# A hybrid decoder layer on one core: new issue orders on all five queues, and the residual's x in the buffer of y

## The chip, the core and the metric

The kernel runs on one core of a Trainium2 chip. The metric is the device time in microseconds (us). The engines are called by their short names: PE (TensorE, matmuls), DVE (VectorE), ACT (ScalarE), POOL (GpSimd) and SP (SyncE, which here only issues DMAs).

## What is computed

One layer of a decoder trunk, 256 tokens of width 1024, all inputs and the output in float32:

```python
h = _rmsnorm(x, norm1_g[i])
proj = h @ w_in[i]
(q_a, k_c, v_c, k_s, v_s, k_w, v_w, g_nsa,
 q_b, k_b, v_b, g_ma, g_mb) = jnp.split(proj, SPLIT_POINTS, axis=-1)
...
y_a = _nsa_mixer(q_a, k_c, v_c, k_s, v_s, k_w, v_w, g_nsa, ...)
y_b = _dilated_mixer(q_b, k_b, v_b)
mixed = jax.nn.sigmoid(g_ma) * (y_a @ w_o_a[i]) + jax.nn.sigmoid(g_mb) * (y_b @ w_o_b[i])
x = x + mixed @ w_out[i]
h2 = _rmsnorm(x, norm2_g[i])
x = x + jnp.square(jax.nn.relu(h2 @ w_up[i])) @ w_down[i]
```

The first mixer attends over compressed, selected and windowed keys, the second over dilated keys; both are causal.

## The kernel before

**Pieces of weights.** Every weight is loaded in float32 pieces of 128 x 768 (384 KB; those of `kv_w` are 128 x 840, 420 KB) by `load_to` (L303 to L317), the first four (`kv_c`) from ACT's DMA queue, all others from SP's. `split_to` then makes two halves of each piece: a high half `wh`, which is a cast to the reduced type of the matmul (on ACT, L345; for piece 0 on DVE, L349), and a low half `wl`, which is what the cast left out (a subtraction on DVE, L350). A product of such a piece with activations, which are kept as two halves in the same way, takes three matmuls: high with high, low with high, high with low (L468 for the very first chunk, L479 to L481 for the other projections, L983 to L985 in `mm3` for gates, output projections and the MLP). So each piece costs one DMA, one ACT cast and one DVE subtraction before PE can use it.

**The start.** x comes in four parts, `xg0` to `xg3` (L314), with the gains of the first norm in front of `xg0`. `scale_x` (L412 to L416) makes the two halves of the scaled x, `hT0` on ACT (L415) and `hT1` on DVE (L416), one chunk `k` of 128 features at a time. `setup` (L422 to L448) squares x on ACT (L426, `sx`), adds the squares on POOL (L428), sums over features on PE (L432) and raises to the power -0.5 on POOL (L436, `rs`); the factor `rs` is applied to what the projections give, not to x. POOL also multiplies the rotary tables by the gains of the heads (L444 `ropeg`, L447). While x is on its way, PE runs ten warm-up matmuls on a tile of `ones` (L408), which POOL sets (L403).

**The middle and the end.** Until about 250 us the projections, both mixers and the gates are interleaved. The attention transposes its probabilities on PE (L709) into a high half (`phi`, ACT) and a low half (`plo`, DVE L714), read by L721 and L723. Each mixer writes into `y` (made at L1052); its last readers are the halves `yb` (ACT L959, DVE L960). Then x is needed a second time, for the residual: `x1` (made at L1100, one load of 1 MB at L1101) is read and rewritten by L1116, and L1117 and L1118 make the halves of `h2` from it. The up- and down-projection fill the rest, and L1175 to L1177 write the result.

**Who decides the order.** `ORDER` holds one list for each engine: numbers of instructions in the order in which they were written in the program, with `a+n` for a run of n of them. `issue_order` ties each engine's instructions together in that order; it adds no semaphore, so an engine takes its instructions in the listed order and each waits only for its own data. A DMA stands in the list of the queue that issues it. `once` makes a tile in the wrapper `Own`, which gives each tile its own buffer, whatever tag it is called with:

```python
    def tile(self, shape, dt, name, **_):
        self.n += 1
        return self.pool.tile(shape, dt, name=name, tag=f"{name}{self.n}", bufs=1)
```

In SP's list numbers 0 to 3 are the four parts of x, 4 to 7 the pieces of `kv_s`, 9, 16, 19 and 20 those of `kv_w`, 8 the identity matrix, 10 `gr` and 11 `rope` (gains and rotary table), 12 to 15, 17 and 18 small constants and masks, 21 to 103 further pieces, 104 the load of `x1`, 105 and on the pieces of the gates' and MLP's weights still to come.

Of the kernel before, what the change touches and what calls it, by code (L numbers as in the profile page):

```python
# [11 lines left out]
F32 = mybir.dt.float32  # L12
# [7 lines left out]
S = 256  # L20
# [100 lines left out]
1 0 2 4 3 9+2 104 15 13 12 16 11 19 14 20 18 5 17 6 8 7 21+83 105+60 166 165 167+4 172 171 173+5 179 178  # L121
180+4 185 184 186+4 191 190 192+5 198 197 199+2""",
    "ACT": """
# [15 lines left out]
474 473 475+3 479 478 481 480 482 484 483 485+3 489 488 491 490 492 494 493 495+3 499 498 501 500 502+38""",  # L139
    "DVE": """  # L140
# [20 lines left out]
635+2 634 637+4 643 641 644 642 645+4 650+2 649 652+2""",  # L161
    "PE": """
# [1124 lines left out]
```

## Time and profile before

| what | us |
| --- | --- |
| median of 3 runs | 458.88 (458.87 to 458.94) |
| the profiled execution | 458.8 |
| its span | 457.0 |
| PE busy | 445.6 (98%) |
| DVE busy | 358.0 (78%) |
| ACT busy | 284.2 (62%) |
| POOL busy | 83.7 (18%) |

All times inside the trace count from the start of the span. The span is a little shorter than the time of the execution, which holds what lies around it. The mean clock granted to PE is 0.993 of full speed. Busy shares are averages over the whole span; the windows further down split them by stage. A matmul is shown with its whole duration although the next one starts before it ends, so a busy PE can still be slower than it might be.

### The profile page before, as it was taken

The page shows a single profiled execution, that of the slowest core. Times are in us where ns is not written, and L with a number is a line of the kernel's source. Part 1 is how long each engine was busy: PE and PEld are TensorE (multiplying, and loading weights), DVE is VectorE, ACT ScalarE, POOL GpSimd, SP SyncE. Part 2 cuts the span into 40 slices and gives each one's busy share as a digit, 9 for nine tenths or more (in the row PEclk, how much of TensorE's full clock was granted, in tenths as well). Part 3 has the DMA queues.
Part 4 walks back from the last instruction along what each step waited for, and adds up shares of the span by engine and source line. Part 5 has one row for each costly group of instructions (what it writes and reads, how often), then busy time and mean ns, then how long its engine had stood idle before and what let it go on. Part 6 is the DMA issues. An engine that isn't in the chain of part 4 may idle for free.

```text
span 457.0 us, 9071 instructions
## 1 busy us (share of the span) xinstructions
PE 445.6 (98%) x3413; PEld 431.1 (94%) x3413; DVE 358.0 (78%) x654; ACT 284.2 (62%) x622; POOL 83.7 (18%) x92
## 2 busy tenths in 40 slices
PE   4999999999999999999999999999999999999996
PEld 4999899899999999898999999999999999999996
DVE  3989999999999998899999886886856654555440
ACT  4855677678999778876775555665665634433330
POOL 2712121313041000200000001796322300000000
PEclk9799999999999999999999999999999999999999
DMA  8974586725535522541521647666666667677620
GB/s 304 367 244 146 154 287 181 236 89 167 157 105 141 171 70 71 175 140 68 162 82 42 199 128 231 201 193 186 205 184 195 183 187 210 185 216 199 179 78 13
DMA packets 29484, 76.92 MB, mean 168 GB/s; under 512 B 3664, under 2 KB 5120, under 8 KB 29312
## 3 DMA queue, kind: packets, MB, share of 16 engines
q1 hardware_dynamic: 28864, 74.77, 54.7%
q10 hardware_dynamic: 576, 1.57, 1.0%
q8 instruction: 27, 0.44, 0.4%
q14 instruction: 17, 0.14, 0.1%
HBM read 75.28 MB, written 1.05 MB: 167 GB/s over the span
## 4 chain that ended last, share of the span: by engine, by line
PE 93%; DVE 2%; ACT 2%; DMA 2%; issue 0%; ACTq 0%
PE acc L983 19%; PE acc L985 19%; PE acc L984 19%; PE acc L480 6%; PE acc L481 6%; PE acc L479 6%; PE tp L709 3%; PE acc L468 2%; DMA raw<-in_kv_c 2%; PE sp L754 1%; PE pvo L721 1%; ACT wh L345 1%; PE pvo L723 1%; PE tp L552 1%; PE dsp L920 1%; PE hacc L615 1%
## 5 line engine op out<-in xcount | busy, mean ns | idle before, releaser
L350 DVE TENSOR_TENSOR wl<-raw,wh 128x768 fp32r<-128x768 f32 (+2 forms) x183 | 177.6, 979 | 61.7 <-ACT wh L345 57.2
L345 ACT CAST wh<-raw 128x768 fp32r<-128x768 f32 (+1 forms) x182 | 149.6, 833 | 102.1 <-PE acc L984 74.5
L983 PE MATMUL acc<-u,wh 128*128 128x256 f32 x256 | 71.6, 280 | 0.0
L984 PE MATMUL acc<-u,wh 128*128 128x256 f32 x256 | 71.6, 280 | 0.0
L985 PE MATMUL acc<-u,wl 128*128 128x256 f32 x256 | 71.5, 279 | 0.0
L984 PE MATMUL acc<-h,wh 128*128 128x256 f32 x256 | 69.0, 280 | 0.0
L983 PE MATMUL acc<-h,wh 128*128 128x256 f32 x256 | 69.0, 279 | 0.0
L985 PE MATMUL acc<-h,wl 128*128 128x256 f32 x256 | 66.1, 279 | 0.0
L480 PE MATMUL acc<-wl,hT 128*128 128x384 f32 (+1 forms) x164 | 55.1, 350 | 0.3 <-DVE wl L350 0.3
L479 PE MATMUL acc<-wh,hT 128*128 128x384 f32 (+1 forms) x164 | 54.7, 348 | 0.0
L481 PE MATMUL acc<-wh,hT 128*128 128x384 f32 (+1 forms) x164 | 54.6, 347 | 0.0
L1159 POOL TENSOR_TENSOR r<-r 128x256 f32<-128x256 f32 x32 | 27.7, 866 | 128.7 <-ACT r L1158 127.5
L985 PEld LDWEIGHTS acc<-u,wl 128*128 128x128 f32 x256 | 48.2, 188 | 0.0
L983 PEld LDWEIGHTS acc<-u,wh 128*128 128x128 f32 x256 | 48.1, 188 | 0.0
L984 PEld LDWEIGHTS acc<-u,wh 128*128 128x128 f32 x256 | 48.1, 188 | 0.0
L983 PEld LDWEIGHTS acc<-h,wh 128*128 128x128 f32 x256 | 47.6, 188 | 0.0
L984 PEld LDWEIGHTS acc<-h,wh 128*128 128x128 f32 x256 | 47.4, 188 | 0.0
L985 PEld LDWEIGHTS acc<-h,wl 128*128 128x128 f32 x256 | 45.8, 188 | 0.0
L502 POOL TENSOR_TENSOR st<-st,nhalf 128x6 f32<-128x6 f32 (+1 forms) x16 | 21.6, 1348 | 92.8 <-DVE st L501 65.7
L984 PE MATMUL acc<-hT,wh 128*128 128x256 f32 x128 | 36.1, 293 | 0.0
L985 PE MATMUL acc<-hT,wl 128*128 128x256 f32 x128 | 35.9, 293 | 0.0
L983 PE MATMUL acc<-hT,wh 128*128 128x256 f32 x128 | 35.1, 290 | 0.0
(212 smaller groups left out, 986.9 us busy)
## 6 DMA issues: line engine op xcount, KB each, us to landing
raw<-in_cells SPq DMA_DIRECT2D x128, 384.0 KB, 3.4
raw<-in_cw SPq DMA_DIRECT2D x10, 384.0 KB, 3.2
raw<-in_q_a SPq DMA_DIRECT2D x8, 384.0 KB, 3.8
raw<-in_q_b SPq DMA_DIRECT2D x8, 384.0 KB, 3.4
raw<-in_k_b SPq DMA_DIRECT2D x8, 384.0 KB, 3.2
raw<-in_v_b SPq DMA_DIRECT2D x8, 384.0 KB, 3.1
raw<-in_kv_w SPq DMA_DIRECT2D x4, 420.0 KB, 6.7
raw<-in_kv_c ACTq DMA_DIRECT2D x4, 384.0 KB, 7.0
```

The source lines that it names most:

```text
L345: nc.scalar.copy(hi[:, :m], src)
L350: nc.vector.tensor_sub(lo[:, :m], src, f(hi[:, :m]))
L468: nc.tensor.matmul(acc[t][:, :n], hT[h][:, k, t * 128:(t + 1) * 128], w[:, kk * n:(kk + 1) * n], start=h == 0 and k == 0 and w is hi, stop ...
L479: nc.tensor.matmul(o, hT[0][:, k, ts], hi[:, c], start=k == 0, stop=False)
L480: nc.tensor.matmul(o, hT[0][:, k, ts], lo[:, c], start=False, stop=False)
L481: nc.tensor.matmul(o, hT[1][:, k, ts], hi[:, c], start=False, stop=k == 7)
L502: nc.gpsimd.tensor_tensor(st[:, 1, :h], st[:, 0, :h], nhalf[:, :h], op=OP.pow)
L709: nc.tensor.transpose(pt[0:rows, i * 128:(i + 1) * 128], s, ident)
L983: nc.tensor.matmul(o, hi, a[0][k], start=start, stop=False)
L984: nc.tensor.matmul(o, hi, a[1][k], start=False, stop=False)
L985: nc.tensor.matmul(o, lo, a[0][k], start=False, stop=stop)
L1159: mul = nc.gpsimd.tensor_mul(r, r, r)
```

## The change

Two lines of `hybrid_layer` give `y` and `x1` one buffer, by taking them from the pool itself with one tag; and all five lists of `ORDER` are replaced by other permutations of the same instructions.

```diff
-    st_["y"] = once([128, 8, S], F32, "y")
+    st_["y"] = big.pool.tile([128, 8, S], F32, name="y", tag="y", bufs=1)
...
-    x1 = big.tile([128, 8, S], F32, name="x1", tag="y", bufs=1)
+    x1 = big.pool.tile([128, 8, S], F32, name="x1", tag="y", bufs=1)
```

```diff
     "SP": """
-1 0 2 4 3 9+2 104 15 13 12 16 11 19 14 20 18 5 17 6 8 7 21+83 105+60 166 165 167+4 172 171 173+5 179 178
-180+4 185 184 186+4 191 190 192+5 198 197 199+2""",
+0+5 9 8 11 10 12 16 19 14 17+2 13 20 15 5+3 21+80 104 101+3 105+60 166 165 167+4 172 171 173+5 179 178 180+4
+185 184 186+4 191 190 192+5 198 197 199+2""",
     "ACT": """
-0+4 6 10 13 9 4+2 7+2 11 16 15 14 17 12 19+2 25+4 18 21 47 22 24 35 48 36 23 49 38 41 37 58 42 29+2 32+2 43
...
+0+4 6 4+2 9 13 7+2 10 14 11 16 15 12 17 20 25 19 26+3 18 21+2 35+2 23 50 24 38 51+2 47 58 32 54 48+2 37 43
...
     "POOL": """
-28 25 2 15 14 0+2 7 3+3 11+2 10 9 8 6 13 18 17 16 19+3 23+2 22 26+2 34+2 38 37 40 29 39 30 33 31 36 32 42 41
...
+0+3 14+2 25 28 7 9 3 8 4 13 5 11 10 12 6 19 18 17 16 20+2 24 22+2 27 34+2 26 37 29 38 40 39 30 33 36 31+2
...
```

What the numbers at the start of these lists are. SP: the load of `x1` moves from the eighth place to the 102nd, just before the last three pieces that are loaded ahead of the MLP's; `xg0` goes ahead of `xg1`, `xg3` ahead of the first piece of `kv_s`, and the identity, `rope` and `gr` come earlier. ACT: behind its four loads (0 to 3) stands the cast of the second `kv_c` piece (6) in both; before, the square of `xg1` (10), the cast of the third piece (13), the square of `xg0` (9) and then the scalings of x (4, 5, 7, 8) follow; after, the scalings 4 and 5, the square of `xg0`, the cast of the third piece, the scalings 7 and 8, the square of `xg1`. DVE: the first two halves `hT1` come before the low half of the third piece, no longer behind it. POOL: `nhalf` and `ones` (0, 1) come first, before the other memsets, and the products of `ropeg` (8, 9, 13) alternate with the adds of the squares (3, 4, 5), behind which they all stood before. PE: the ten warm-up matmuls and the first chunk's products stay first; products of the first token half and the second are grouped otherwise, and the sums L432 move from the places 43 to 57 to the places 84 to 87. In the up-projection PE's new list runs straight as written, where the old one still exchanges neighbours; the down-projection is straight in both. In between, every list is permuted throughout. One example, which the prediction takes up: the low half `plo` whose reader is PE's instruction number 705 moves ten places ahead in DVE's list (from 349 to 339), and that reader 89 places ahead in PE's (from 1172 to 1083).

## Rows read from the trace of the kernel before

**Rows 1.** Waits of PE; columns: engine, line, awaited, us in total, times, longest.

```profile
PE acc L468 <- ACT hT L415: 4.1, 1, 4.1
PE acc L408 <- POOL ones L403: 2.4, 1, 2.4
PE tp L536 <- ACT kc L646: 0.3, 1, 0.3
```

**Rows 2.** Windows; columns: stretch, length, busy PE, PEld, DVE, ACT, POOL, PEclk, DMA, GB/s.

```profile
2.45:7.03 4.58, 4.58 (x20) 4.34 (x20) 1.59 (x3) 1.28 (x1) 0.05 (x1) 1.00 0.95 336
7.03:11.12 4.09, 0.00 (x1) 0.01 (x1) 1.91 (x3) 3.18 (x6) 0.51 (x2) 0.89 1.04 413
11.12:17.20 6.08, 6.08 (x19) 5.74 (x20) 6.08 (x8) 6.03 (x12) 4.16 (x3) 0.51 1.04 391
17.20:20.00 2.80, 2.80 (x20) 2.80 (x18) 2.80 (x4) 1.44 (x2) 1.56 (x2) 1.00 1.00 357
...
20.00:180.00 160.00, 159.23 (x1072) 149.84 (x1072) 152.10 (x324) 119.92 (x316) 29.66 (x26) 1.00 0.54 164
180.00:250.00 70.00, 69.79 (x560) 65.54 (x559) 65.59 (x142) 50.61 (x119) 2.81 (x3) 1.00 0.36 108
```

**Rows 3.** Costliest groups; columns: line, engine, operation, count, busy us, mean ns, idle before.

```profile
L984 PE MATMUL acc<-u,wh 128*128 128x256 f32 x256 | 71.6, 280 | 0.0
...
L984 PE MATMUL acc<-hT,wh 128*128 128x256 f32 x128 | 36.1, 293 | 0.0
```

**Rows 4.** Timeline of the first 24 us; columns: start, us, engine, line, operation, idle before.

```profile
0.72 0.98 POOL L870 MEMSET pc<- 48x512 f32 x2 [0.29 <-POOLq L1277]
...
6.98 0.19 POOL L440 COPY g<-xg 128x8 f32<-128x8 f32 x1 [4.58 <-DMA xg<-in_xg]
...
7.52 0.83 ACT L345 CAST wh<-raw 128x768 fp32r<-128x768 f32 x1 [3.39 <-DMA raw<-in_kv_c]
8.26 0.63 ACT L426 ACTIVATE sx<-xg 128x512 f32<-128x512 f32 x1
8.39 0.96 DVE L350 TENSOR_TENSOR wl<-raw,wh 128x768 fp32r<-128x768 f32 x1 [1.75 <-ACT wh L345]
...
9.30 0.83 ACT L345 CAST wh<-raw 128x768 fp32r<-128x768 f32 x1 [0.42 <-DMA raw<-in_kv_c]
...
10.16 0.96 DVE L350 TENSOR_TENSOR wl<-raw,wh 128x768 fp32r<-128x768 f32 x1 [0.82 <-ACT wh L345]
10.57 0.89 ACT L415 ACTIVATE hT<-xg 128x256 fp32r<-128x256 f32 x2
...
11.12 3.13 PE L468 MATMUL acc<-wh,hT 128*128 128x384 f32 x8 [4.09 <-ACT hT L415]
...
14.05 1.16 PE L468 MATMUL acc<-wl,hT 128*128 128x384 f32 x3
...
15.71 1.46 POOL L428 TENSOR_TENSOR sx<-sx,sx 128x512 f32<-128x512 f32 x1 [1.23 <-ACT sx L426]
15.95 2.99 DVE L350 TENSOR_TENSOR wl<-raw,wh 128x768 fp32r<-128x768 f32 x2
```

**Rows 5.** Tile y, its last reader on DVE: ns min/median/max, first and last start.

```profile
L960 DVE SCALAR_TENSOR_TENSOR yb<-y,yb x2: 415/420/426, 238.8 to 244.9; 128x256 fp32r<-128x256 f32 x2
```

**Rows 6.** Tile x (`x1` in the program): first reader, and its load to landing.

```profile
L1116 DVE TENSOR_TENSOR x<-acc,x x8: 424/425/426, 262.9 to 274.0; 128x256 f32<-128x256 f32 x8
...
DMA to landing us min/median/max: 8.9/8.9/8.9
```

**Rows 7.** Timeline of DVE and of PE, 255 to 261 us: the piece loaded next.

```profile
255.51 0.95 DVE L350 TENSOR_TENSOR wl<-raw,wh 128x768 fp32r<-128x768 f32 x1
...
260.46 0.40 PE L985 MATMUL acc<-mT,wl 128*128 128x256 f32 x2
```

**Rows 8.** Timeline of DVE and of PE, 186 to 189 us: the low half `plo`.

```profile
186.26 0.68 DVE L714 TENSOR_TENSOR plo<-tp,phi 128x512 fp32r<-128x512 f32 x1
...
188.61 0.42 PE L723 MATMUL pvo<-plo,vSW 128*64 128x512 f32 x1
```

More of the change, by code (lines that the diff above doesn't have):

```diff
@@ L120 @@
     "SP": """
-1 0 2 4 3 9+2 104 15 13 12 16 11 19 14 20 18 5 17 6 8 7 21+83 105+60 166 165 167+4 172 171 173+5 179 178
-180+4 185 184 186+4 191 190 192+5 198 197 199+2""",
+0+5 9 8 11 10 12 16 19 14 17+2 13 20 15 5+3 21+80 104 101+3 105+60 166 165 167+4 172 171 173+5 179 178 180+4
+185 184 186+4 191 190 192+5 198 197 199+2""",
     "ACT": """
[15 rows of a table removed]
-474 473 475+3 479 478 481 480 482 484 483 485+3 489 488 491 490 492 494 493 495+3 499 498 501 500 502+38""",
-    "DVE": """
[20 rows of a table removed]
-635+2 634 637+4 643 641 644 642 645+4 650+2 649 652+2""",
-    "PE": """
[60 rows of a table removed]
-2575+17 2597 2592+3 2598 2595 2599+20 2620 2619 2621+767""",
[15 rows of a table added]
+484 483 485+3 489 488 491 490 492 494 493 495+3 499 498 501 500 502+38""",
+    "DVE": """
[20 rows of a table added]
+637+4 643 641 644 642 645+4 650+2 649 652+2""",
+    "PE": """
[49 rows of a table added]
+1907+280 2188+17 2187 2205+1183""",
     "POOL": """
-28 25 2 15 14 0+2 7 3+3 11+2 10 9 8 6 13 18 17 16 19+3 23+2 22 26+2 34+2 38 37 40 29 39 30 33 31 36 32 42 41
-45+5 44 50+5 56 55 57+4 62 61 63+11 43 74+14""",
+0+3 14+2 25 28 7 9 3 8 4 13 5 11 10 12 6 19 18 17 16 20+2 24 22+2 27 34+2 26 37 29 38 40 39 30 33 36 31+2
+41+14 56 55 57+4 62 61 63 65 64 66 68 67 69+19""",
 }
```

177 rows, old and new, of the table ORDER are left out of this document.

## The prediction, made before the changed kernel was run

> **What bounds the kernel now.** I read the waits of TensorE (PE) first [rows 1]: its only long waits are 2.4 us for a memset before the warm-up matmuls and 4.1 us for `hT` before the first projection matmul; no other is longer than 0.3 us. Then the windows [rows 2]: from 11.12 on PE is busy almost throughout (159.23 of 160.00 us between 20 and 180, 69.79 of 70.00 between 180 and 250). So what is issued first decides the start, and afterwards only a change of pace or a new hold can move the end. The tail after the last matmul holds the same instructions in both kernels, and I price it at no change.
>
> Busy is not the same as full pace, though. VectorE (DVE) is busy 152.10 of 160.00 us between 20 and 180 [rows 2], and matmuls that read fresh halves are a little longer there: 293 ns with `hT` against 280 with `u` [rows 3]. With 128 calls in each of three such lines (the other two 293 and 290), that is 128 x (13 + 13 + 10) ns = 4.6 us of small holds inside "busy". This is where a new order can gain or lose besides the start.
>
> The profiled execution reports 458.8 us for a span of 457.0; the median of the runs is 458.88, which is 0.08 more. The sum is made on 458.8. A measurement of this kernel tells changes above 0.2%, 0.92 us, from none.
>
> **Part 1, the start.** Before, ScalarE (ACT) waits until 7.52 for the second `kv_c` piece, casts it, squares `x` (0.63), waits 0.42 for the third piece, casts it (0.83), squares again and scales the first chunk of `x` only at 10.57; PE starts at 11.12 [rows 4]. In the new ACT list both first `hT` scalings stand directly behind the first cast. Consecutive ACT instructions overlap slightly, the next starting about 0.1 before the end shown, as the square at 8.26 did. So the scaling starts at 8.26, and PE starts as long after it as before, 11.12 - 10.57 = 0.55: at 8.81 instead of 11.12, a gain of **2.31**. The data for it is there: `xg0`, which also holds the gains, had landed by 6.98, where a POOL copy waited for it, and is now issued ahead of `xg1`. The squares, the third cast and POOL's adds that move behind the scaling feed `rs`, which no matmul of the first projection reads.
>
> **Part 2, three stumbles.** In 11.12 to 17.20 PE issues 19 matmuls [rows 2], one every 6.08 / 19 = 0.32. The first eight reach from 11.12 to the start of the ninth at 14.05 [rows 4]: 2.93 - 8 x 0.32 = **0.37** lost, at the matmuls that read the low half `hT1`, which DVE makes after the low half of the third piece (10.16 + 0.96 = 11.12). DVE's list now has the first pair of `hT1` ahead of that, right behind the low half of the second piece (8.39 + 0.96 = 9.35). I take the 0.37 as gained; the bounds are 0 and 0.37.
>
> **Part 3, the clock.** The granted clock is 1.00 during the warm-up, 0.89 over the idle stretch 7.03 to 11.12, 0.51 from 11.12 to 17.20 and 1.00 after [rows 2]; 0.51 is the lower of the two levels, 1.2 GHz. The lower level costs 6.08 x (1 - 0.51) = 2.98 us. POOL's new list puts the `ones` memset, for which PE waited 2.4 us [rows 1], second instead of seventh. POOL's memsets start at 0.72 [rows 4]; behind one short one it is done by about 1.0, an estimate. The warm-up then starts about 1.4 earlier, and with its 4.58 ends at 5.6; PE then idles 5.6 to 8.81, 3.2 us against 4.09 before. No row shows whether the shorter gap spares the drop, so its worth lies between 0 and **2.98**. I take 0: a gap of the same kind, only a fifth shorter, is nearest to the one shown. It stays the largest term that may turn out better.
>
> **Part 4, x for the residual.** The 1 MB load of `x1` leaves SP's list at 7.52 and moves ahead of the last three pieces before the mixers end. At the 391 GB/s of 11.12 to 17.20 [rows 2] its megabyte takes 2.7 us, so the loads queued behind it (`kv_w1` and on) land up to 2.7 earlier. Before, that was hidden: DVE was busy 6.08 of 6.08 and 2.80 of 2.80 there. Now it covers the earlier start of PE, so I book no gain; without it the start would be partly given back. At the new place the load waits for the last reader of `y`, DVE's `yb` at 244.9 + 0.42 = 245.3, and lands 2.7 to 8.9 later (its price alone at that rate, and issue to landing of the copy before): 248.0 to 254.2. Its first reader is at 262.9, a margin of 8.7 us or more [rows 5, 6]. The three `cells` pieces behind it in SP's queue wait with it: at 384 KB, 1.0 us each by the same rate, the first is there by 249.0 to 255.2. DVE makes its low half at 255.51, and PE reads that at 260.46 [rows 7], 4.0 after DVE's end at 256.46; even the late bound, with a cast like the 0.83 of rows 4 and the 0.95 of DVE behind it, gives 257.0 and leaves 3.5. Price 0.
>
> **Part 5, the other 430 us.** All five lists are permuted far into the up-projection. No instruction is added or removed, and PE's work is the same. The bounds are a gain of the 4.6 us of holds [rows 3] and a loss, worked out as rival C. I take 0, since the holds come from DVE, whose sum of work is unchanged and which has only 160.00 - 152.10 = 7.9 us of idle to give.
>
> **Sum:** 458.8 - 2.31 - 0.37 = 456.1, and with the 0.08 to the median **456.2 us**.
>
> **Rivals.** A: the clock does not drop, or DVE's work arrives better ordered in the middle. The first alone gives 456.2 - 2.98 = 453.2; half the holds alone, 2.3, give 453.9. I price this case at **453.5**. For it speaks that both sources are real time in the rows; against it that nothing in DVE's load is removed.
>
> B: DVE cannot follow. It was idle 1.75 before 8.39 and 0.82 before 10.16 [rows 4]; its first work still waits for the same landings, and only most of that 0.82, about 0.6, is recovered. If the holds of the middle are all DVE's, PE falls back on DVE's schedule and 458.88 - 0.6 = **458.3** remains, no change by measurement. What feeds this: POOL's `ropeg` products now stand between its adds and so fall into the time in which DVE makes low halves. Beside a POOL add that starts at 15.71, two DVE low halves take 2.99 where one alone takes 0.96 [rows 4], so about 1.1 lost to one meeting; two or three such meetings moved into the start eat the 2.31. By the Trainium skill, page "SBUF — State Buffer", section "🔬 SBUF: two separate sides", VectorE and GpSimd share one pair of ports as an exclusive lock, and the one that starts first keeps it for its whole instruction. By that rule, with which the row of 2.99 agrees, the total lost is the same as before and only its place moves.
>
> C, the other sign: PE's list runs ahead of DVE's at the attention. The low half `plo` of the transposed probabilities is done at 186.26 + 0.68 = 186.94 and read at 188.61, a slack of 1.67 [rows 8]. In the new lists it stands 10 places earlier on DVE, worth 10 x 152.10 / 324 = 4.7, but its reader stands 89 places earlier on PE, worth 89 x 69.79 / 560 = 11.1 [rows 2]. PE would get there 11.1 - 4.7 - 1.67 = 4.7 too soon, and it starts 2.7 earlier besides while DVE gains 0.6 at the start: 6.8 to make up. DVE can make it up from its 7.9 us of idle, if the new order fills nearly all of it. If it fills only 2.0, PE is held 4.8 and the time is 456.2 + 4.8 = **461.0**. The deciding point is 4.1 us of idle filled, at which the wait equals the 2.7 gained; below it the kernel is slower. Against it: places are not time, and other waits before 180 may already have been shortened by the same reordering.
>
> SP held up by the shared buffer would also make it slower, but only if `y`'s last reader came over 3.5 us later than now; I give that no chance of its own.
>
> **Chances.** Forecast 0.54, own range 454.9 to 457.6 (the 0.37 and part of a meeting on one side, half of the clock's cost on the other); A 0.20; B 0.11; C 0.15. Faster by over 0.2% (below 457.96) takes the forecast and A: 0.74; within 0.2% B: 0.11; slower C: 0.15. The range reaches over A's 453.2 to B's upper end, 459.0, and leaves out C and a little below: **453.0 to 459.0**.
>
> **What would show it.** Right: first `hT` on ACT near 8.3 and PE's first L468 near 8.8; a low clock stretch of about 6 us following it; no wait of L1116 for a DMA; SP's `x1` issue at 243 to 246; PE still without long waits. Wrong: PE starting at 9.5 or later because the second `kv_c` piece lands later; PE waits for `plo`, `phi` or `wl` of some us between 140 and 200 (C); PE pitch above 0.17 around 17 to 40 with DVE full (B); or no 0.51 stretch at all (A).

## The result: slower, and the profile after

The changed kernel takes **463.99 us** in the median (462.46 to 464.5, 4 runs) against 458.88 (458.44 to 458.94): ratio 1.0108, 95% interval 1.0083 to 1.0132, slower by 1.1%. The forecast was 456.2 with a range to 459.0. The profiled execution took 464.11 with a span of 462.1, so the two profiles differ by 5.1 us of span. All lines of the program have moved up by 11 (L468 is now L457, L350 is L339, L428 is L417).

The busy line of the page after, then its waits of PE, in the columns of [rows 1]:

```profile
PE 449.1 (97%) x3413; PEld 433.0 (94%) x3413; DVE 360.2 (78%) x654; ACT 284.5 (62%) x622; POOL 86.4 (19%) x92
```

```profile
PE acc L457 <- ACT hT L404: 3.4, 1, 3.4
PE acc L469 <- DVE wl L339: 2.5, 1, 2.5
PE hacc L602 <- DVE blk L589: 1.7, 1, 1.7
PE acc L397 <- POOL ones L392: 1.0, 1, 1.0
PE pvo L710 <- DVE plo L703: 0.2, 1, 0.2
```

Two of [rows 1] are shorter, and two new waits on DVE have come, 4.2 us together. The windows, in the columns of [rows 2], say when:

```profile
9.00:12.00 3.00, 3.00 (x11) 3.00 (x11) 2.60 (x6) 3.00 (x6) 0.00 (x0) 0.50 1.04 392
...
20.00:60.00 40.00, 35.82 (x210) 33.83 (x209) 35.43 (x67) 20.68 (x39) 9.44 (x10) 0.96 0.48 149
...
24.90:28.30 3.40, 3.34 (x10) 3.20 (x11) 2.85 (x4) 2.87 (x4) 0.00 (x0) 0.50 0.02 5
```

Between 20 and 60 PE is idle for 4.2 us, and behind the first of the two waits it ran 3.4 us at the granted clock of 0.50, the lower level, 1.2 GHz. The timeline of 18 to 27 us shows what it waited for (columns as in [rows 4]):

```profile
18.02 2.10 POOL L417 TENSOR_TENSOR sx<-sx,sx 128x512 f32<-128x512 f32 x1
20.07 0.64 POOL L436 TENSOR_TENSOR ropeg<-ropec,gr 48x128 f32<-48x128 f32 x1
20.32 4.59 DVE L339 TENSOR_TENSOR wl<-raw,wh 128x840 fp32r<-128x840 f32 x1
20.67 1.29 POOL L417 TENSOR_TENSOR sx<-sx,sx 128x512 f32<-128x512 f32 x1
21.92 2.09 POOL L433 TENSOR_TENSOR ropeg<-rope,gr 128x256 f32<-128x256 f32 x3
24.96 0.72 PE L469 MATMUL acc<-wl,hT 128*128 128x420 f32 x1 [2.48 <-DVE wl L339]
```

One low half takes 4.59 us; the next of its shape takes 1.02. It begins inside POOL's small product (48 partitions), POOL then runs an add and three products without a gap to 24.01, and DVE ends 0.9 behind them (24.91). This row, with PE's wait and the low clock behind it, is the largest loss.

**How late PE is, by amount of work.** Both kernels give PE the same matmuls, so I count each at the distance to the next that is usual for its shape in the trace of before (the lower quarter), and note when a given amount had been started. This is worked out from the traces, and a different order shifts it by some tenths. The kernels of the other columns come below.

```
                    later than the kernel before, us (negative: earlier)
PE work  time       after  small_    changed_   new_start_  products_  light_   light_
done us  before            product_  products_  old_        later      before   after
                           last      later      middle
 12       22.3      -3.0   -2.9      -2.5       -0.4        -1.5       -0.6     -4.5
 20       30.9      +1.7   -1.7      -2.3       -0.3        -1.3       -0.6     -4.0
 28       39.7      +1.3   -2.2      -2.7       -0.3        -1.3       -0.6     -4.4
 60       74.8      +3.0   -0.4      +0.1       -0.1        -0.9       -1.9     -3.3
160      188.2      +5.2   +1.9      +2.4       -0.1        -1.0       -2.3     -2.5
240      281.7      +4.3   +0.9      +1.5       -0.0        -0.7       -2.8     -3.8
end      452.9      +5.1   +1.7      +2.2       -0.3        -1.2       -1.9     -3.2
```

In its own time the changed kernel is 3.0 us ahead at 19 us, loses 4.7 by 33 us (the 4.59 row, the wait, the low clock), and from 41 to 286 us 3.0 more. The last 0.8 comes behind 286 us; the last section says what it is. So two things had to be explained, and the experiments take them one by one.

### The profile page after: what moved, and what is told of

Read it like the earlier page. It is cut to its first block, busy times and chain, and to the rows that moved or that the text cites. A ratio compares the mean times of both kernels' runs of the same rounds, so it can differ in the third digit from the quotient of the medians.

```text
span 462.1 us, 9059 instructions
## 1 busy us (share of the span) xinstructions
PE 449.1 (97%) x3413; PEld 433.0 (94%) x3413; DVE 360.2 (78%) x654; ACT 284.5 (62%) x622; POOL 86.4 (19%) x92
## 4 chain that ended last, share of the span: by engine, by line
PE 84%; DVE 7%; ACT 2%; issue 1%; POOL 0%; DVEq 0%
PE acc L973 19%; PE acc L972 18%; PE acc L974 18%; PE acc L469 5%; PE acc L468 5%; PE acc L470 5%; PE tp L698 2%; PE sp L743 1%; DVE wl L339 1%; PE pvo L710 1%; PE pvo L712 1%; PE dsp L909 1%; DVE b L584 1%; PE hacc L602 1%; PE sa L743 1%
## 5 line engine op out<-in xcount | busy, mean ns | idle before, releaser
L339 DVE TENSOR_TENSOR wl<-raw,wh 128x768 fp32r<-128x768 f32 (+2 forms) x183 | 182.6, 1005 | 64.0 <-ACT wh L334 63.5
L974 PE MATMUL acc<-h,wl 128*128 128x256 f32 x256 | 71.5, 280 | 0.0
L973 PE MATMUL acc<-h,wh 128*128 128x256 f32 x256 | 71.5, 280 | 0.0
L972 PE MATMUL acc<-h,wh 128*128 128x256 f32 x256 | 70.9, 279 | 0.0
L469 PE MATMUL acc<-wl,hT 128*128 128x384 f32 (+1 forms) x164 | 56.1, 354 | 2.5 <-DVE wl L339 2.5
L470 PE MATMUL acc<-wh,hT 128*128 128x384 f32 (+1 forms) x164 | 55.6, 352 | 0.0
L468 PE MATMUL acc<-wh,hT 128*128 128x384 f32 (+1 forms) x164 | 55.0, 349 | 0.1
L1148 POOL TENSOR_TENSOR r<-r 128x256 f32<-128x256 f32 x32 | 30.1, 943 | 132.9 <-ACT r L1147 132.9
L974 PEld LDWEIGHTS acc<-h,wl 128*128 128x128 f32 x256 | 48.0, 188 | 0.0
L972 PEld LDWEIGHTS acc<-h,wh 128*128 128x128 f32 x256 | 48.0, 188 | 0.0
L973 PEld LDWEIGHTS acc<-h,wh 128*128 128x128 f32 x256 | 48.0, 188 | 0.0
L491 POOL TENSOR_TENSOR st<-st,nhalf 128x6 f32<-128x6 f32 (+1 forms) x16 | 23.3, 1459 | 92.9 <-DVE st L490 72.5
```

The source lines that it names most:

```text
L339: nc.vector.tensor_sub(lo[:, :m], src, f(hi[:, :m]))
L468: nc.tensor.matmul(o, hT[0][:, k, ts], hi[:, c], start=k == 0, stop=False)
L469: nc.tensor.matmul(o, hT[0][:, k, ts], lo[:, c], start=False, stop=False)
L470: nc.tensor.matmul(o, hT[1][:, k, ts], hi[:, c], start=False, stop=k == 7)
L491: nc.gpsimd.tensor_tensor(st[:, 1, :h], st[:, 0, :h], nhalf[:, :h], op=OP.pow)
L972: nc.tensor.matmul(o, hi, a[0][k], start=start, stop=False)
```

## The experiments

**The changed kernel again**, unchanged, for a second trace.

> The changed kernel once more, for a second trace. Theory P (POOL's adds and products of the rotary table shut DVE out at 14 to 24 us: one low half took 4.59 us instead of 1.02, PE waited 2.5 us for it and then ran at the lower clock for 3.3 us): one DVE subtraction of 3 us or more between 15 and 27 again, PE's wait for a low half of 1.5 to 4 us, time 462 to 465. Theory O (the new order of the middle itself makes PE wait on DVE, whatever POOL does): the same time, but the long subtraction may be missing.

463.15 us (460.88 to 465.58, 6 runs), ratio 1.0094 (1.0062 to 1.0125). The long low half is there again (4.58, beginning at 20.18, again inside the small product), and PE's wait is 2.5. In this execution, 460.88, the granted clock was 1.00 throughout: PE came back from its wait at 24.81, against 24.96 in the first trace, and was level with the kernel before at 31 us, where the first trace was 1.7 late. So the lower clock behind the wait costs about 1.5 in those executions in which it is granted.

**Where POOL's products stand.** Three kernels change the head of POOL's list in the changed kernel, and nothing else (3, 4, 5 are the adds, 8 to 12 the large products, 13 the small one, 6 `rs`):

```diff
 changed:             0+3 14+2 25 28 7 9 3 8 4 13 5 11 10 12 6 ...
+tables_behind_rs:    0+3 14+2 25 28 7 3+4 9 8 13 11 10 12 ...
+pool_as_before:      0+3 14+2 25 28 7 3+3 11+2 10 9 8 6 13 ...
+small_product_last:  0+3 14+2 25 28 7 9 3 8 4+2 11 10 12 6 13 ...
```

> The changed kernel with POOL's six products of the rotary table moved behind the adds and behind rs; all else as changed. Theory P: no DVE subtraction over 2.5 us before 28 us, PE's wait for a low half under 0.7 us, no lower clock at 25 us, so the 4.7 us that PE lost between 19 and 33 us are mostly back: 459 to 460.5. Theory O: the stall goes but PE falls behind later all the same, 462.5 to 464.

> The changed kernel with POOL's head in the order of the kernel before (three adds, five products in a run, rs, the sixth), the memsets still first. Theory P: the products still run before 24 us, beside DVE's low halves, but in one run; DVE loses 2 to 4 us to them somewhere between 14 and 24, 461 to 464. If only the alternation of adds and products does the harm, the loss is under 1.5 us and the time 459 to 460.5. Theory O: 463 to 464.5.

> The changed kernel with one POOL instruction moved: the small product of the rotary table (48 partitions, L436) goes from between the last two adds to the end of POOL's head, behind rs. In both traces of the changed kernel the DVE low half that took 4.6 us began while this small product ran, and in tables_behind_rs a tiny DVE operation of 2.53 us did too. Theory L (a DVE operation that begins in the small product loses every turn until POOL's run ends): no DVE operation over 2.3 us before 30 us, PE's wait for a low half 0.6 or less instead of 2.5, time 460 to 461.5. Theory R (any run of an add and three products shuts DVE out for 4 us): a subtraction of 3.5 us or more stays, 462.5 to 464.

Measured: tables_behind_rs 461.31, 1.0051 (1.0033 to 1.0069); pool_as_before 460.69, 1.0033 (1.0016 to 1.0049); small_product_last 460.63, 1.0033 (1.0019 to 1.0048). All three gain against the changed kernel, so POOL's head costs something; theory O alone is out. The third is the telling one: one small instruction moved behind the others gives 2.5 to 3.4 us (463.15 and 463.99 against 460.63). In its trace the same low half reads so, though an add and a product of POOL run beside it:

```profile
20.69 2.11 DVE L339 TENSOR_TENSOR wl<-raw,wh 128x840 fp32r<-128x840 f32 x1
```

The expectation of pool_as_before (461 to 464, if DVE loses 2 to 4) was too high: its run of five products lets DVE in at every turn (5.57 for the five, and no DVE operation over 1.6 beside them). And tables_behind_rs missed its 459 to 460.5. It has a second lockout of the same kind: a DVE operation on two columns takes 2.53 us there, beginning in the small product, and PE then waits 2.1 for the gates. That explains a part of the miss at most: changed_products_later (further down) has no such operation, and takes 460.98. The timelines of POOL and of DVE in tables_behind_rs:

```profile
29.44 0.45 POOL L436 TENSOR_TENSOR ropeg<-ropec,gr 48x128 f32<-48x128 f32 x1
29.86 2.12 POOL L433 TENSOR_TENSOR ropeg<-rope,gr 128x256 f32<-128x256 f32 x3
...
29.48 2.53 DVE L428 TENSOR_SCALAR nrs<-rs 128x2 f32<-128x2 f32 x1
```

**The shared buffer alone.** The kernel before with the two lines of the change and SP's load moved:

```diff
-1 0 2 4 3 9+2 104 15 13 ... 21+83 105+60 ...
+1 0 2 4 3 9+2 15 13 ... 21+80 104 101+3 105+60 ...
```

> The kernel before with only the shared buffer of y and x1, and SP's load of x1 moved to its new place. Theories P and O: nothing on the path changes, 458.0 to 459.3; weights land up to 2.7 us earlier at the start, x1 lands 3 to 9 us after 245 and L1116 does not wait for it. Theory S (the shared buffer is the cost): 460.5 or more, with L1116 or a cast near 250 waiting for a DMA.

459.80, 1.0015 (1.0004 to 1.0026): slower by at most a quarter of a per cent, 0.5 above the 458.0 to 459.3 that theories P and O had, and below the 460.5 of theory S. The new waits of PE are three for a low half, 1.0 in all, and two of 0.4, for a cast and for `hT1`. Between 214 and 283 us, where the load now stands, PE falls back by only 0.2; from 236 on it waits for nothing there, and L1116 does not wait for the load. So theory S, the shared buffer as the cost, is out; the change of SP's order may cost some tenths in these other lists.

**The new start on the old middle.** Both kernels start from the kernel before. The first takes SP's list, 22 places of ACT's, 17 of DVE's and POOL's memsets from the change (and the shared buffer); the second moves two scalings on ACT.

```diff
 new_start_old_middle, ACT:
-0+4 6 10 13 9 4+2 7+2 11 16 15 14 17 12 19+2 25+4 ...
+0+4 6 4+2 9 13 7+2 10 14 11 16 15 12 17 20 25 19 26+3 ...
 scaling_first_only, ACT:
-0+4 6 10 13 9 4+2 7+2 ...
+0+4 6 4+2 10 13 9 7+2 ...
```

> The kernel before with the shared buffer, SP's new list, the first 22 places of ACT's and the first 17 of DVE's new lists, and POOL's memsets first; everything behind these in the old order, PE's list wholly old. Theory M (the new start gains about 2 us and the new middle loses about 3 against the old): 456 to 457.7, no wait for blk at 50. Theory D (DVE's work is the limit up to 250, whatever the start): what is gained at the start is gone by 100 us, 458.5 to 459.5.

> The kernel before with one pair moved in ACT's list: the first two scalings of x come directly behind the cast of the second piece; nothing else. If xg0 is there at 8.3 and nothing else holds: PE starts at 8.8 instead of 11.1, and by theory M 456.2 to 457.5 if DVE's idle time in the start gives way, by theory D 458.5 to 459.3 since DVE's first halves come no earlier.

458.77, 1.0009 (0.9992 to 1.0025), and 460.51, 1.0038 (1.0023 to 1.0053). Two waits of PE in new_start_old_middle, and POOL's products beside which they fall:

```profile
PE acc L480 <- DVE wl L350: 1.7, 3, 1.2
...
PE acc L468 <- DVE hT L416: 0.7, 1, 0.7
```

```profile
16.31 5.56 POOL L444 TENSOR_TENSOR ropeg<-rope,gr 128x256 f32<-128x256 f32 x5
```

By the table it is only 0.4 ahead at 22 us. Behind that it neither gains nor loses. Theory D holds for the start. The pair of scalings alone is worse than nothing, outside both expectations: PE starts at 8.78, but the squares and the cast of the third piece come later on ACT, so DVE's third low half starts at 10.40 instead of 10.16 [rows 4], `hT1` follows it at 11.27 and meets a POOL add, and PE waits 2.8 for `hT1`.

**One misplaced pair in the middle.** On pool_as_before, `blk0`, which PE reads first, is made ahead of `blk1`:

```diff
 DVE:
-... 28 33+2 29 40 47 35 50+2 48 52 49 30 ...
+... 28+2 33+2 40 47 30 50+2 48 52 49 35 ...
 ACT:
-... 39 34 31 42 ...
+... 39 31 34 42 ...
```

> pool_as_before (460.7) with blk0, which PE reads first, made ahead of blk1: six instructions exchanged on DVE and two on ACT, at 46 to 52 us. Theory M (single badly placed instructions of the new middle make PE wait): PE's wait for blk falls from 1.7 to 0.4 or less and 1 us or more of it stays to the end, 459.0 to 459.8. Theory D (DVE's sum of work sets the pace): the wait goes but PE is as late at 150 us as before the edit, 460.4 to 461.

459.48, 1.0015 (1.0006 to 1.0025), against 460.69. By the time theory M is right (459.0 to 459.8) and theory D is not (460.4 to 461). The traces say otherwise. The wait for `blk` (1.7) is gone, but another takes its place:

```profile
PE hacc L604 <- DVE wl L339: 0.9, 1, 0.9
```

At 75 us PE stands as in pool_as_before (74.49 and 74.53), as it does at 190 us (190.19 and 190.23), and at 283 us it is 0.2 ahead. So up to there the wait gave next to nothing that lasts. What the two traces differ by at their ends (1.4) arises behind 280 us, where both kernels have the same order; it is the pace told of in the last section. Each kernel has executions near 459.5 and near 460.7, pool_as_before one and four of its five, blk0_first eight and two of its ten. Why blk0_first is mostly at the lower value is not shown, so theory M is not quite out.

**DVE made lighter.** In the kernel before and in small_product_last the low half of each weight piece becomes a copy; taking out the high half is left out:

```diff
-            nc.vector.tensor_sub(lo[:, :m], src, f(hi[:, :m]))
+            nc.vector.tensor_copy(lo[:, :m], src)
```

> The kernel before with every weight's low half made by a copy of the raw piece instead of a subtraction: one source instead of two, so that part of the computation (taking out the high half) is left out and DVE has less to do; order and data flow are unchanged. Theory D (DVE's work sets PE's pace between 15 and 250 us): the copy takes 0.5 to 0.7 instead of 0.96, DVE gets idle time of 15 us or more between 36 and 250, and the time falls by 2 to 5 us, 454 to 457.

> small_product_last (the changed kernel, 460.6) with the same copy in place of the subtraction. Theory D: with DVE out of the way the new start is kept, so this kernel comes out 1.5 to 3 us faster than light_before. Theory O (the new middle is slower in itself, by waits of PE on ACT, on itself or on loads): it stays 1 to 2 us slower than light_before.

456.89, 0.9952 (0.9937 to 0.9967), and 455.89, 0.9933 (0.9917 to 0.9948). The copies take 0.58 instead of 0.96. The groups and the windows of light_before:

```profile
L350 DVE CAST wl<-raw 128x768 fp32r<-128x768 f32 x178 | 101.6, 579 | 64.5 <-PE acc L985 59.8 <-DMA raw<-in_kv_c 2.6 <-DMA raw<-in_cells 1.4
```

```profile
36.00:250.00 214.00, 213.82 (x1552) 202.22 (x1553) 178.94 (x444) 161.70 (x419) 26.23 (x22) 1.00 0.47 140
```

With DVE idle for 35 us of that stretch, both orders gain 2 us or more, and the new one, 1.7 slower with the subtraction (460.63 against 458.96 for the kernel before beside it), is now 1.0 faster, less than the 1.5 to 3 of theory D. Now the new start is kept up to 40 us (-4.4). That is more than the 2.7 booked. The clock may have a part in it, which was not separated: from 12 to 16 us it was 1.00 in light_after, and 0.50 in light_before. But the new middle still loses: from work 28 to 240 light_after falls back by 0.6 while light_before gains 2.2. So DVE's load explains why the start is given back, and not why the new middle is worse; neither theory had both.

**The small product moved in.** On new_start_old_middle, the reverse of small_product_last:

```diff
-0+3 14+2 25 28 7 3+3 11+2 10 9 8 6 13 ...
+0+3 14+2 25 28 7 3+3 13 11+2 10 9 8 6 ...
```

> new_start_old_middle (458.8) with one POOL instruction moved the other way: the small product, 48 partitions, from the end to between the last add and the run of five products, at about 16.4 us, where DVE's low half of 16.56 began. Theory L (a DVE operation that begins in the small product is shut out until POOL's run ends): one DVE operation of 3.5 us or more between 15 and 22, PE waits 2 to 3 us more, 461 to 463. If the small product has nothing to do with it: no such operation, 458.3 to 459.3.

463.50, 1.0092 (1.0072 to 1.0113), 4.7 us more than without and 0.5 above theory L's range; PE waits 2.2 longer for low halves. The timeline of POOL and DVE:

```profile
16.71 1.13 POOL L447 TENSOR_TENSOR ropeg<-ropec,gr 48x128 f32<-48x128 f32 x1 [0.34 <-DMA ropec<-in_ropec]
17.45 4.10 DVE L416 SCALAR_TENSOR_TENSOR hT<-xg,xg,hT 128x256 fp32r<-128x256 f32 x1
17.81 3.45 POOL L444 TENSOR_TENSOR ropeg<-rope,gr 128x256 f32<-128x256 f32 x5
```

A scaling of 0.47 takes 4.10: from inside the small product to the end of POOL's run. The five products need 0.69 each; in new_start_old_middle, where DVE gets its turns, the same five take 5.56.

**48 partitions, or a short product?** In two kernels the small product runs over 128 partitions, with the same 128 elements in each; it reads the first table of `rope`, so the rotation of the compressed keys by their own table is left out.

```diff
-        tab = const.tile([48, 2, 64], F32, name="ropeg5")
-        nc.gpsimd.tensor_mul(tab, ropec, gr[0:48, :, 5])
-        ropeg[5] = tab
+        tab = const.tile([128, 2, 64], F32, name="ropeg5")
+        nc.gpsimd.tensor_mul(tab, rope[:, 0], gr[:, :, 5])
+        ropeg[5] = tab[0:48]
```

> small_product_early (463.5), but the small product runs over 128 partitions instead of 48, with the same 128 elements in each; it takes the first table of rope in place of ropec, so the compressed keys' rotation is computed from the wrong table. Theory N (the 48 partitions make the lockout): no DVE operation over 2.5 us between 15 and 24, time 458.3 to 460. Theory B (any short product at the head of a run does it): one DVE operation of 3.5 us or more, 462 to 464. If no DVE operation begins while it runs, the run says nothing.

> The changed kernel (463 to 464) with the small product over 128 partitions in the same way, at its own place. Theory N: the 4.6 us low half is gone and the time is that of small_product_last, 459.6 to 461.4. Theory B: 462.5 to 465.

458.92, 1.0001 (0.9984 to 1.0018), and 460.08, 1.0026 (1.0012 to 1.0040): the lockout is gone in both, with the instruction in its harmful place. In both a low half does begin inside it; first small_product_128, then changed_128:

```profile
16.28 0.65 POOL L447 TENSOR_TENSOR ropeg<-rope,gr 128x128 f32<-128x128 f32 x1
16.89 6.17 POOL L444 TENSOR_TENSOR ropeg<-rope,gr 128x256 f32<-128x256 f32 x5
...
16.53 1.21 DVE L350 TENSOR_TENSOR wl<-raw,wh 128x768 fp32r<-128x768 f32 x1
```

```profile
19.62 0.64 POOL L436 TENSOR_TENSOR ropeg<-rope,gr 128x128 f32<-128x128 f32 x1
20.22 2.09 POOL L417 TENSOR_TENSOR sx<-sx,sx 128x512 f32<-128x512 f32 x1
```

```profile
19.86 1.28 DVE L339 TENSOR_TENSOR wl<-raw,wh 128x840 fp32r<-128x840 f32 x1
```

In changed_128 it is the low half that took 4.59, and it begins as far into the small product as there (0.24 and 0.25 us): 1.28 instead of 4.59. So the lockout comes and goes with the place of this one instruction, in both directions, and goes when it covers 128 partitions. The edit also changes the table that it reads; that this plays no part was not tried by itself.

Not every POOL operation on 48 partitions does it. In the trace of the changed kernel a low half that begins inside a power of one column takes its usual time:

```profile
86.07 1.66 POOL L640 TENSOR_TENSOR kcs<-kcs,nhalf 48x1 f32<-48x1 f32 x1 [1.47 <-DVE kcs L639]
...
86.38 0.94 DVE L339 TENSOR_TENSOR wl<-raw,wh 128x768 fp32r<-128x768 f32 x1
```

**Where the new middle loses.** Two kernels change over at 66 us: new_until_66 is small_product_last with the old order behind, old_until_66 is new_start_old_middle with the new order behind (PE's list cut at place 330).

> small_product_last (the changed kernel with its small product last, 460.6) with the new lists only for what runs in the first 66 us (330 places of PE's list, 100 of DVE's, 69 of ACT's, 24 of POOL's) and everything behind in the old order. Theory T1 (the middle's loss of about 3 us arises half before 66 us, at the first compression block, and half behind it, in the attention): 0.4 us ahead of the kernel before at 66 us and so at the end, 458.3 to 459.2. Theory T2 (all of it arises behind 66): 457.5 or less. Theory T3 (all of it arises before): 460 to 461.

> new_start_old_middle (458.8) with the new lists for what runs after 66 us (behind 330 places of PE's list, 104 of DVE's, 72 of ACT's, 24 of POOL's). Theory T1: 1 to 1.5 us are lost between 100 and 160 us, 459.8 to 460.6. Theory T2: 461.5 or more. Theory T3: 458.5 to 459.2.

> The changed kernel with POOL's five large products behind rs and the small one last: tables_behind_rs (461.3) without its second lockout, in which a tiny DVE operation took 2.53 us and PE waited 2.1 for gates. Theory L: no DVE operation over 2 us before 36, the wait for gates gone, and by the middle's loss of about 3 us 459 to 460.3, still not faster than the kernel before. If the middle only loses because the start upsets it: 457.5 to 458.5, as products_later.

459.14, 1.0001 (0.9991 to 1.0011); 461.92, 1.0057 (1.0036 to 1.0077); and changed_products_later (POOL's head `... 7 3+4 9 8 10+4`) 460.98, 1.0037 (1.0020 to 1.0055). new_until_66 has theory T1's time, but not its path: T1 had PE 0.4 ahead at 66 us, and it is 0.3 late there and 1.1 late at 70, so 0.9 is lost at the change-over itself. Behind that the old order loses nothing (+1.1 at 76 us, +0.9 at 283). old_until_66 has theory T2's time (461.5 or more). Its trace is of its slowest execution (463.79), which was 3 us late by 30 us already; the other three (461.63 to 461.94) have no trace. In it about 1.5 us are lost at the change-over, where PE waits for `vq`:

```profile
PE tp L525 <- DVE vq L517: 1.2, 1, 1.2
```

From there to 287 us it loses 1.3, which is the new order's loss there in small_product_last and changed_products_later as well (-0.4 to +0.9, +0.1 to +1.5). So each seam costs about as much as the splice was to measure, and the two times do not decide between T1, T2 and T3; the stretches away from the seams count. changed_products_later shows the same loss with no lockout: no DVE operation over 2 us before 36 us, and still 460.98, above its 459 to 460.3 (its wait for the gates is still 1.1). And pool_as_before, with the old head of POOL's list and the new start, takes 460.69, where new_start_old_middle takes 458.77. So the middle is worse in itself. Of the loss of about 3 us, 1.7 to 2.8 lie before 75 us and about 1.3 behind, by the table's columns of the three kernels with the new order throughout.

**A version that beats both.** On new_start_old_middle, POOL's products behind `rs`, the small one last:

```diff
-0+3 14+2 25 28 7 3+3 11+2 10 9 8 6 13 ...
+0+3 14+2 25 28 7 3+4 9 8 10+4 ...
```

> new_start_old_middle with POOL's products of the rotary table moved behind rs (the small one last), out of the stretch in which PE waits for low halves (15 to 22 us). If DVE's meetings with POOL there are what gives the new start back: PE's waits for wl fall from 1.7 to 0.7 or less and the time to 457 to 458. If the meetings only move to 23 to 28 us: 458.5 to 459.3.

**457.61** (456.89 to 457.8), ratio **0.9964** (0.9950 to 0.9978), 0.36% faster than the kernel before. Its waits of PE:

```profile
PE acc L468 <- ACT hT L415: 3.2, 1, 3.2
PE acc L408 <- POOL ones L403: 1.0, 1, 1.0
PE acc L468 <- DVE hT L416: 0.8, 1, 0.8
PE acc L480 <- DVE wl L350: 0.5, 2, 0.3
PE tp L536 <- ACT kc L646: 0.3, 1, 0.3
```

The waits for `wl` fall from 1.7 to 0.5. DVE's meetings with POOL have moved to 22 to 29 us, where PE does not wait for them, and 1.2 us of the new start reach the end. The small product now stands last, and a low half that begins in it at 27.41 takes 1.23.

## Why the prediction was wrong

**The steps that failed.** The sum carried the 2.68 us of Parts 1 and 2 to the end as a gain. It put the meetings of DVE with POOL in the start at nothing; only rival B had them, at 1.1 each. And it took the other 430 us at 0. In their place the runs showed: with the old middle the 2.68 are all but gone by 22 us (new_start_old_middle, 458.77), one meeting cost 4.7 with the low clock behind it (3.6 in the second trace, where the clock stayed at 1.00), and the new middle lost 3.0.

**Parts 1 and 2 were right in their times and wrong as terms of the sum.** The first `hT` starts at 7.97 (8.26 forecast), PE's first projection matmul at 8.53 (8.81), and PE was 3.0 us ahead at 19 us against 2.68 in the sum. What failed is Part 4's "Now it covers the earlier start of PE": DVE, beside POOL's products, does not make the halves in time for the earlier start, and PE waits 1.7 and 0.7 for them. With a lighter DVE the start is kept up to 40 us (light_after), and with POOL's products elsewhere 1.2 of it reach the end (products_later).

**Part 3, the clock**: no number was booked. The lower level came in the first trace (0.50 from 9 to 12) and not in the second (1.00), which is 0.5 further ahead at 19 us. In the kernel before the bound of 2.98 was not a cost: of its executions beside the experiments, the eight at a mean granted clock of 1.000 took 458.85 to 459.61, and the 23 at 0.991 or 0.992 took 458.44 to 459.91. That PE waits for DVE there if the clock does not drop is likely, and not shown: no trace of such an execution was kept.

**Part 4 was right in its sum and wrong in its premise.** The load of `x1` started at 239.86 and landed 4.8 later, before `y`'s last reader (L949, at 249.3):

```profile
L1105 DVE TENSOR_TENSOR x<-acc,x x8: 416/420/425, 268.2 to 279.4; 128x256 f32<-128x256 f32 x8
...
L1090 SPq DMA_DIRECT2D x<-in_xg x1: 327/327/327, 239.9 to 239.9; - x1
...
DMA to landing us min/median/max: 4.8/4.8/4.8
```

So it does not wait for `y`. SP held it for the dilated keys:

```profile
SPq L1090 <- PE dsp L912: 3.1, 1, 3.1
SPq L1090 <- DVE dk L547: 2.1, 1, 2.1
```

In the program as built `x1` lies where `hT0` and the dilated keys were, and `y` lies elsewhere: the common tag does not put the two tiles in one buffer, as the section on the change and Part 4 took it. It changes nothing in the time: the first reader comes 23 us behind the landing.

**Part 5 failed**: "the other 430 us" priced at 0 lost 3.0 us (+1.3 to +4.3 in the table). The step that failed is "I take 0, since the holds come from DVE, whose sum of work is unchanged". The sum is unchanged, and the loss came all the same. That the new middle is worse in itself is shown (changed_products_later, and pool_as_before against new_start_old_middle). Which of its exchanges does it is not: taking out the largest wait gained 0.2 by 283 us, and a lighter DVE did not cure it. This stays open.

**Rival B** had the cause of the rest, with the wrong price: "about 1.1 lost to one meeting". That POOL's large products fall into DVE's time was not new either; they ran beside its low halves before:

```profile
18.44 5.24 POOL L444 TENSOR_TENSOR ropeg<-rope,gr 128x256 f32<-128x256 f32 x5 [1.26 <-DMA rope<-in_rope]
```

New was the small product with a run of POOL's behind it. B's end value, 458.3 if DVE cannot follow, is near what new_start_old_middle shows (458.77). But that one meeting cost 3.6 us (4.59 - 1.02), and PE's wait and the low clock behind it made 4.7. By the Trainium skill, page "SBUF — State Buffer", section "🔬 SBUF: two separate sides", whichever of the two starts first has the shared ports for its whole instruction, and the other blocks. The rows agree for POOL's products on 128 partitions: beside the run of five in new_start_old_middle DVE got its turns, and operations of 0.95, 0.47 and 1.02 took 1.48, 0.95 and 1.56. They do not agree for the one on 48: there DVE lost every turn of up to five further instructions.

**Rival C** had the sign (461.0, slower) and not the place: the wait for `plo` is 0.2.

## What to carry to other kernels

Where two engines contend, the order in the cheap engine's list can cost more than the work in question (here one instruction of 0.64 us cost 2.5 to 3.4 by its place): look in the trace for one instruction that takes several times the mean of its group, and see what ran beside it. An earlier start is worth what the next engine in the chain can follow; ask for its idle time in that stretch before booking the gain. And a reordering is not free because the sums are the same: set the two traces side by side by amount of work, and the stretch that loses shows itself. A splice of the old and the new order helps less than it seems, since the seam has a cost of its own (here 0.9 and about 1.5).

## What the runs showed of the chip that was not expected

- A DVE operation that begins while POOL's product of 48 partitions and 128 columns runs stays shut out until POOL's run ends: 4.59, 4.58, 4.10 and 2.53 us in four traces, where 1.02, 1.02, 0.47 and 0.15 to 0.17 are usual. Over 128 partitions the two take turns. No partition counts other than 48 and 128 were tried, and a power on 48 partitions and one column did not do it.
- The pace of the same matmuls differs between executions by 0.9% although the granted clock reads 1.00: from one start to the next it is 117.8 ns or 116.7. The window of 300 to 450 us in the first and in the second trace of the changed kernel:

```profile
300.00:450.00 150.00, 150.00 (x1275) 149.95 (x1275) 92.73 (x113) 74.27 (x121) 32.93 (x36) 1.00 0.66 183
```

```profile
300.00:450.00 150.00, 150.00 (x1287) 149.94 (x1286) 91.03 (x112) 73.28 (x119) 31.24 (x35) 1.00 0.65 180
```

  12 matmuls of 0.117 us are 1.4 us in this stretch alone, so differences of that size between two traces are read from the stretch in question, not from the end. The last 0.8 of the 5.1 us between the two profiles is of this kind. From 350 to 450 us seven of the ten traces with the new order there show the slower pace, and one of the nine with the old order. So the order may have a part in it; that was not tried, and what sets the pace is open.
